# Four plain rows instead of six in a seven-product SwiGLU layer, with weight sums made by accumulating transfers

## The chip, the core and the metric

The kernel runs on one core of a Trainium2 chip. A core has five engines with queues of their own: TensorE (PE) multiplies, VectorE (DVE) and ScalarE (ACT) work on elements, GpSimd (POOL) here does little but issue transfers, and SyncE (SP) only issues transfers. The metric is device microseconds (us) from start to end; less is better. A measurement of this kernel can tell about 0.2% from no change, some 2.2 us.

## The reference, cut to what matters

One decoder layer is computed for 544 tokens (512 of a prompt, 32 of a decode step): a half-step SwiGLU feed-forward layer, a token mixer, and a second feed-forward layer of the same form with other weights. The change touches the two feed-forward layers only.

```python
def half_ffn(x, g_pre, g_post, w_gate, w_up, w_down):
    h = rmsnorm(x, g_pre)
    u = jax.nn.silu(h @ w_gate) * (h @ w_up)
    return x + 0.5 * rmsnorm(u @ w_down, g_post)
```

D_MODEL is 1024 (8 blocks of 128) and FFN_DIM is 2816 (22 blocks of 128), all in float32.

## The kernel before, in words

Everything lies transposed: features on the 128 partitions, the 544 tokens along the free dimension. A "row" is one block of 128 of the 2816 hidden features, so u has 22 rows. A float32 product is done in three passes of a reduced format: each operand is split into a high part (a cast on ACT) and a low part (a subtraction on DVE), and high x high, high x low and low x high are accumulated in PSUM.

Each feed-forward layer (`ffn`) makes its 22 rows in two ways.

*Plain rows* (PLAIN = 6 of them, rows 0 to 5): gate and up are two products over 8 blocks of the model dimension, for two token halves of 288 and 256 tokens. One such job (gate or up, one half) is 8 x 3 = 24 matmuls into a buffer `acc` of PSUM (three buffers), and a row has four jobs. `gate_out` multiplies the gate by the tokens' reciprocal norm `r` and applies silu; `upper_out` multiplies the up product by `r` and by the gate, and in the kernel before splits the result into the high and low parts that the down projection needs (lines 614 to 617), in SBUF.

*Pairs of rows* (`quadrants`, rows 6 to 21, so 8 pairs): gate and up of two rows together form a 2 x 2 block product (gate and up on one side against two halves of the model dimension, and two halves of 272 tokens on the other), done with seven products instead of eight (PRODUCTS, in the order 1, 5, 6, 2, 7, 3, 4). A product is 2 x 12 matmuls of 272 columns (two rows, 4 blocks, 3 passes), a pair 7 x 24 = 168. Four of the seven left factors are sums of the raw weights g0, g1 (the two halves of gate) and u0, u1 (of up): s3 = g0 + u0 for product 7, and u0 + u1, then + g0, then + g1 for products 5, 6 and 3. DVE makes all four, with `plus`. The right factors are seven combinations of the negated, normalised h, split into high and low parts (tiles `t` and `h`), made once for each layer by `right_parts` and `factors`. Before, ACT first scales X in place by the gain (line 422) and DVE by -r (line 429), and the parts come out of X.

The first pair must wait for its right factors. `ffn` therefore makes them in steps between the jobs of the plain rows (`steps`, `making`), and runs the last three jobs of the plain rows between the first products of the first pair (`beside`). So the plain rows are also the time in which DVE and ACT prepare the pairs. Weights are split one tile of 128 x 1024 at a time into a pool of three buffers; raw weights come by SP into a pool `raw` of two buffers, and the up weights of a pair into `rawx` or into the second half of X, in turn.

KEEP = 8 rows are multiplied with the down weights by seven products as well (`seven_down`), and the 14 others by three plain passes. Of the rows made by pairs, the first four pairs (rows 6 to 13) go out to DRAM (`u_keep`, by POOL) and come back later for `seven_down`.

The order on each engine is set when the program is built, by a list scheduler that goes by its own estimates of durations; each engine then runs its list strictly in order, so an instruction that waits holds up all behind it. A transfer's waits are held by the queue of the engine that issues it: POOL's list is in order too.

Of the kernel before, what the change touches and what calls it, by code (L numbers as in the profile page):

```python
# [39 lines left out]
WK = 4  # L40
# [3 lines left out]
PLAIN = 6  # L44
KEEP = 8

# [158 lines left out]
class _Builder:  # L205
# [202 lines left out]
    def u_tiles(self, li, ctx):  # L408

        t = ctx.enter_context(self.tc.tile_pool(name="u%d" % li, bufs=1)).tile([128, 2 * PLAIN, T], F32R, name="u%d" % li)  # L410
        return {m: (t[:, 2 * m, :], t[:, 2 * m + 1, :]) for m in range(PLAIN)}


    def right_parts(self, hs, gi, pool, behind):


        nc = self.nc
        X = self.X
        for k0 in range(0, KT, WK):
            with self.tc.issue_after(behind):  # L420
                for k in range(k0, k0 + WK):
                    nc.scalar.activation(out=X[:, k, :], in_=X[:, k, :], func=AF.Copy,
                                         scale=self.gain[:, gi * KT + k:gi * KT + k + 1])
            yield
        for half in range(2):
            r = self.rs(hs, half).unsqueeze(1).to_broadcast([128, WK, self.hw(half)])
            for k in range(0, KT, WK):
                x = X[:, k:k + WK, self.cols(half)]
                nc.vector.scalar_tensor_tensor(out=x, in0=x, scalar=-1.0, in1=r, op0=ALU.mult, op1=ALU.mult)
            yield  # L430
        h8 = self.h8, "h8"
        yield from self.factors({1: (pool, "t"), 5: (pool, "t"), 6: (pool, "t"), 2: h8, 7: h8, 3: h8, 4: h8})

    def factors(self, places):
# [3 lines left out]
        n11, n12, n21, n22 = (self.X[:, k:k + WK, c:c + HALF] for k in (0, WK) for c in (0, HALF))  # L438
# [81 lines left out]
    def quadrants(self, raws, small, put, beside, making):  # L520
# [4 lines left out]
        s3 = flat[:, 0:1024].rearrange("p (k m) -> p k m", k=WK)  # L525
# [6 lines left out]
        for u in range(PLAIN, KF, 2):  # L532
            (g0, g1), (u0, u1) = ((r[:, 0:WK], r[:, WK:KT]) for r in loaded)
            if PLAIN < u < KF - 2:
# [1426 lines left out]
```

## Time and profile before

| what | us |
|---|---|
| median of three runs | 1120.24 (1119.25 to 1120.26) |
| the profiled execution: its time | 1119.48 |
| the profiled execution: its span | 1117.7 |
| PE busy | 1100.3 (98%) |
| DVE busy | 845.0 (76%) |
| ACT busy | 632.8 (57%) |
| POOL busy | 124.7 (11%) |

In a timeline row the first number is the start in us from the beginning of the span, the second the length; then come engine, line of the program, operation, written tile <- read tiles, shape and count. Short instructions of one engine overlap at their ends, so the cost of one in a busy queue is the distance to the next start. A view of waits names who waited, for whom, the total, how often and the longest.

### The profile page before, as it was taken

To read this page: it belongs to the slowest core of one execution; us is meant where nothing else is said; L and a number is where in the kernel's file an instruction comes from. 1 tells how busy PE (TensorE), PEld (TensorE's weight loads), DVE (VectorE), ACT (ScalarE), POOL (GpSimd) and SP (SyncE) were. 2 spreads that over 40 slices of the span, in tenths; PEclk is the share of its full clock that TensorE was granted. 3 is DMA by queue.
4 is the path that set the end of the run, shared out by engine and by line. 5 is a ranking of instruction groups with operands and counts; after the bars stand their busy time and mean duration, and the time that the engine had idled before them with its cause. 6 is when DMAs were issued, how large, how long until landed. Compare 5 with 4: busy or idle time off the path is not lost.

```text
span 1117.7 us, 21930 instructions
## 1 busy us (share of the span) xinstructions
PE 1100.3 (98%) x8722; PEld 1063.1 (95%) x8722; DVE 845.0 (76%) x1716; ACT 632.8 (57%) x1368; POOL 124.7 (11%) x176
## 2 busy tenths in 40 slices
PE   9999999999999999999999899999999999999997
PEld 8999999999999999899889789999999999999997
DVE  5996787877875799658676478899787788787544
ACT  5844455555554656667564366776454455555444
POOL 0000000000000143521234432000000000000000
PEclk9999999999999999999999999999999999999999
DMA  9442344224245555643355546653333332243272
GB/s 269 143 133 94 116 134 130 80 66 153 71 150 172 153 146 143 189 132 91 92 158 172 170 126 203 203 177 110 114 127 118 132 101 91 89 133 95 82 212 80
DMA packets 150149, 149.47 MB, mean 134 GB/s; under 512 B 5965, under 2 KB 139189, under 8 KB 148512
## 3 DMA queue, kind: packets, MB, share of 16 engines
q1 hardware_dynamic: 135600, 100.55, 30.4%
q0 software_dynamic: 11504, 44.82, 11.9%
q10 hardware_dynamic: 2944, 2.71, 0.9%
q8 instruction: 68, 1.11, 0.4%
q14 instruction: 33, 0.27, 0.1%
HBM read 130.08 MB, written 18.51 MB: 133 GB/s over the span
## 4 chain that ended last, share of the span: by engine, by line
PE 81%; DVE 7%; issue 5%; ACT 3%; DMA 2%; POOL 1%; DVEq 0%; POOLq 0%; ACTq 0%; SPq 0%
PE acc L252 11%; PE acc L253 11%; PE acc L254 11%; PE acc L479 6%; PE acc L477 6%; PE acc L478 6%; PE aux L477 5%; PE aux L479 5%; PE aux L478 5%; PE smp L477 2%; PE smp L479 2%; PE smp L478 2%; DVE wl L241 2%; ACT wh L240 1%; PE smp L1357 1%
## 5 line engine op out<-in xcount | busy, mean ns | idle before, releaser
L240 ACT CAST wh<-raw 128x512 fp32r<-128x512 f32 (+2 forms) x281 | 183.3, 683 | 147.0 <-PE acc L253 62.8
L241 DVE TENSOR_TENSOR wl<-raw,wh 128x512 fp32r<-128x512 f32 (+2 forms) x281 | 209.2, 769 | 48.0 <-ACT wh L240 44.6
L252 PE MATMUL acc<-ha,wh 128*128 128x256 f32 (+1 forms) x576 | 166.3, 289 | 1.2 <-DVE rpost L614 1.2
L253 PE MATMUL acc<-ha,wh 128*128 128x256 f32 (+1 forms) x576 | 165.9, 288 | 0.0
L254 PE MATMUL acc<-ha,wl 128*128 128x256 f32 (+1 forms) x576 | 165.6, 287 | 0.0
L252 PE MATMUL acc<-h,wh 128*128 128x256 f32 (+1 forms) x552 | 164.2, 298 | 0.0
L253 PE MATMUL acc<-h,wh 128*128 128x256 f32 (+1 forms) x552 | 160.8, 292 | 0.0
L254 PE MATMUL acc<-h,wl 128*128 128x256 f32 (+1 forms) x552 | 160.0, 290 | 0.0
L252 PEld LDWEIGHTS acc<-h,wh 128*128 128x128 f32 x552 | 104.6, 190 | 7.7 <-issue 7.1
L252 PEld LDWEIGHTS acc<-ha,wh 128*128 128x128 f32 x576 | 108.8, 189 | 2.3 <-DVE rpost L614 1.4
L254 PEld LDWEIGHTS acc<-ha,wl 128*128 128x128 f32 x576 | 108.9, 189 | 0.0
L253 PEld LDWEIGHTS acc<-ha,wh 128*128 128x128 f32 x576 | 108.8, 189 | 0.1
L253 PEld LDWEIGHTS acc<-h,wh 128*128 128x128 f32 x552 | 104.7, 190 | 0.7 <-issue 0.4
L254 PEld LDWEIGHTS acc<-h,wl 128*128 128x128 f32 x552 | 104.4, 189 | 0.6 <-issue 0.4
L241 DVE TENSOR_TENSOR wl<-X,wh 128x1024 fp32r<-128x1024 f32 x48 | 58.8, 1224 | 26.5 <-ACT wh L240 26.5
L477 PE MATMUL acc<-h,wh 128*128 128x272 f32 x256 | 74.2, 290 | 0.0
L479 PE MATMUL acc<-t,wl 128*128 128x272 f32 x256 | 74.2, 290 | 0.0
L479 PE MATMUL acc<-h,wl 128*128 128x272 f32 x256 | 74.1, 289 | 0.0
L477 PE MATMUL acc<-t,wh 128*128 128x272 f32 x256 | 74.0, 289 | 0.0
L478 PE MATMUL acc<-t,wh 128*128 128x272 f32 x256 | 73.8, 288 | 0.0
L478 PE MATMUL acc<-h,wh 128*128 128x272 f32 x256 | 73.7, 288 | 0.0
L240 ACT CAST wh<-X 128x1024 fp32r<-128x1024 f32 x48 | 50.4, 1049 | 25.8 <-PE aux L478 14.8
(511 smaller groups left out, 3100.3 us busy)
## 6 DMA issues: line engine op xcount, KB each, us to landing
raw<-in_ffn_w_gate_dram SPq DMA_DIRECT2D x20, 1024.0 KB, 5.4
raw<-in_w_in_dram SPq DMA_DIRECT2D x28, 512.0 KB, 4.2
raw<-in_ffn_w_down_dram SPq DMA_DIRECT2D x21, 512.0 KB, 5.3
rawx<-in_ffn_w_up_dram SPq DMA_DIRECT2D x8, 1024.0 KB, 5.4
X<-in_ffn_w_up_dram SPq DMA_DIRECT2D x8, 1024.0 KB, 5.2
raw<-in_ffn_w_down_dram SPq DMA_DIRECT2D x8, 1024.0 KB, 5.7
raw<-in_ffn_w_down_dram SPq DMA_DIRECT2D x21, 384.0 KB, 3.8
raw<-in_w_out_dram SPq DMA_DIRECT2D x7, 1024.0 KB, 5.2
```

The costliest lines, as they stand in the source:

```text
L240: self.nc.scalar.copy(out=high, in_=src)
L241: self.nc.vector.tensor_tensor(out=low, in0=src, in1=high.bitcast(F32), op=ALU.subtract)
L252: nc.tensor.matmul(ps, lhsT=wh, rhs=xh(k0 + k), start=st, stop=False)
L253: nc.tensor.matmul(ps, lhsT=wh, rhs=xl(k0 + k), start=False, stop=False)
L254: self.last_mm = nc.tensor.matmul(ps, lhsT=wl, rhs=xh(k0 + k), start=False, stop=sp).ins
L477: nc.tensor.matmul(ps, lhsT=wh[:, k0 + k, cs], rhs=high[:, k, :], start=st, stop=False, skip_group_check=True)
L478: nc.tensor.matmul(ps, lhsT=wh[:, k0 + k, cs], rhs=low[:, k, :], start=False, stop=False, skip_group_check=True)
L479: self.last_mm = nc.tensor.matmul(ps, lhsT=wl[:, k0 + k, cs], rhs=high[:, k, :], start=False, stop=sp, skip_group_check=True).ins
L1357: nc.tensor.transpose(ps[:, h * 128:h * 128 + 128], kp[:, h * 128:h * 128 + 128], self.ident)
```

## The change

PLAIN goes from 6 to 4, so nine pairs take the place of eight. All four plain rows go out to DRAM as plain float32, half a row at a time: `upper_out` no longer splits its result but hands it to a transfer on POOL's queue (line 619), out of the small two-buffer pool tile `sqe` that the early gate also uses. Rows 0 to 7 (four plain rows and two pairs) now are the KEEP rows, and rows 8 to 13 take the place (`own`) that the plain rows had.

The normalised h gets a place of its own: DVE writes it from X with one operation per block of 128 features (line 423, X times `minus` times `r`), into the memory that later holds rows 8 to 13; ACT's scaling (line 422) is gone, and X keeps the raw input until it is used as a buffer. `r` is one tile for both halves. `minus` is the negated gain, made once on POOL.

Two of the four weight sums move to transfers. u0 + u1: after the load of the up weights, POOL issues a transfer that adds u1 from DRAM onto u0 in SBUF (line 706). s3 = g0 + u0: SP loads g0 into the place of s3 (line 713) and POOL adds u0 from DRAM onto it (line 714), one pair ahead. Both accumulating transfers bring 512 KB and wait on POOL for the load that they add to.

The making of the right factors is cut into three steps beside the plain rows (before, nine), and one step at each product of the first pair (before, all that was left at product 2).

The first place that moves is POOL's list in the first feed-forward layer. Before (x_ffn is the copy of X for the residual; bias_row and windows belong to the attention bias):

```order
L671 DMA x_ffn_586<-X_85 128x2176
L671 DMA x_ffn_586<-X_86 128x2176
L948 DMA bias_row<-xt 4x384
L951 DMA windows<-bias_row 512x1x256
L712 DMA u_keep_1042<-X_85 128x1088 x4
```

And now (u_keep<-sqe is half a plain row going out; the transfers from in_ffn_w_up_dram on this queue are the accumulating ones, X_85 being s3's place and X_86 the up weights of the second pair):

```order
L706 DMA rawx<-in_ffn_w_up_dram 128x4x256
L672 DMA x_ffn_583<-X_85 128x2176
L672 DMA x_ffn_583<-X_86 128x2176
L619 DMA u_keep_396<-sqe 128x288
L714 DMA X_85<-in_ffn_w_up_dram 128x4x256
L619 DMA u_keep_396<-sqe 128x256
L963 DMA bias_row<-xt 4x384
L966 DMA windows<-bias_row 512x1x256
L619 DMA u_keep_396<-sqe 128x288
L619 DMA u_keep_396<-sqe 128x256
L706 DMA X_86<-in_ffn_w_up_dram 128x4x256
```

The second half of row 0 (the 128x256 transfer behind the first one) now stands behind the accumulation onto s3, and both halves of row 1 behind windows.

The second place is DVE's list in the same layer, from row 1 on. Before:

```order
L241 TENSOR_TENSOR wl<-raw,wh 128x1024
L617 TENSOR_TENSOR u_99<-rpost,u_99 128x256
L598 TENSOR_TENSOR sq<-acc,r_460 128x288
L614 TENSOR_TENSOR rpost<-aux,r_460 128x288
L429 SCALAR_TENSOR_TENSOR X_86<-X_86,r_460 128x4x288
L615 TENSOR_TENSOR rpost<-rpost,sq 128x288
```

And now, with the semaphores that each waits for in brackets (DMASW is one of eight that POOL's transfers use in turn; here DMASW7 is the transfer of row 0's second half, DMASW2 that of row 1's first half; the number behind it is the same in all rows and says nothing):

```order
L242 TENSOR_TENSOR wl<-raw,wh 128x1024 [waits DMAHW4_49,Activation_49]
L609 TENSOR_TENSOR sq<-sq,sqe 128x288 [waits Activation_49]
L617 TENSOR_TENSOR sqe<-aux,r 128x288 [waits DMASW7_49,DVE_49]
L617 TENSOR_TENSOR sqe<-acc,r 128x256 [waits DVE_49]
L618 TENSOR_TENSOR sqe<-sqe,sq 128x288 [waits DVE_49]
L618 TENSOR_TENSOR sqe<-sqe,sq 128x256 [waits DVE_49]
L603 TENSOR_TENSOR sq<-acc,r 128x288 [waits PE_49]
L242 TENSOR_TENSOR t<-u,t 128x1088 [waits DMAHW5_49,DMASW1_49,DMAHW6_49,DMASW0_49,Activation_49]
L242 TENSOR_TENSOR wl<-raw,wh 128x1024
L617 TENSOR_TENSOR sqe<-acc,r 128x288 [waits DMASW2_49,DVE_49,PE_49]
```

The up product of row 1 (the two L617 next to each other) now has to wait until row 0's second half has left its buffer for DRAM, and that of row 2 (the last line) until row 1's first half has.

The third place is ACT's list in the first layer. Before, the gate's exponentials of rows 0 and 1 stand together and one table load follows (r_497 is the second half's norm):

```order
L601 ACTIVATE sqe<-sq 128x288
L603 ACTIVATE sqe<-sqe 128x288
L602 ACTIVATE sqe<-sqe 128x288
L279 ACTIVATE r_497<-r_497 128x256
L603 ACTIVATE sqe<-sqe 128x288
L240 CAST wh<-raw 128x1024
L616 CAST u_99<-rpost 128x288
L606 ACT_TABLE_LOAD
```

And now:

```order
L608 ACTIVATE sqe<-sqe 128x288
L611 ACT_TABLE_LOAD
L611 ACTIVATE sq<-sq 128x256
L606 ACT_TABLE_LOAD
L606 ACTIVATE sqe<-sq 128x288
L611 ACT_TABLE_LOAD
L611 ACTIVATE sq<-sq 128x256
L607 ACT_TABLE_LOAD
L607 ACTIVATE sqe<-sqe 128x288
L241 CAST wh<-raw 128x1024
L608 ACT_TABLE_LOAD
L608 ACTIVATE sqe<-sqe 128x288
```

Silu (L611) of the second half and the exponentials of row 1 (L606 to L608) alternate, each with a table load of its own; another load before the next silu makes six where there was one. The second layer has one in both.

The diff, cut to its core:

```diff
-PLAIN = 6
+PLAIN = 4
 KEEP = 8
+OWN = 6
...
-            r = self.rp.tile([128, HA], F32, name="r%d" % half)[:, 0:self.hw(half)]
+            if hs[1 - half][3] is None:
+                self.r = self.rp.tile([128, T], F32, name="r")
+            r = self.r[:, self.cols(half)]
...
+    def right_parts(self, gi, place, pool):
+        nc = self.nc
+        n = place.tile([128, 2 * OWN, T], F32, name="u")[:, 0:KT]
+        def scaled(k0):
+            for k in range(k0, k0 + WK):
+                nc.vector.scalar_tensor_tensor(out=n[:, k, :], in0=self.X[:, k, :],
+                                               scalar=self.minus[:, gi * KT + k:gi * KT + k + 1], in1=self.r,
+                                               op0=ALU.mult, op1=ALU.mult)
+        scaled(0)
+        yield
+        h8 = self.h8, "h8"
+        making = self.factors({1: (pool, "t"), 5: (pool, "t"), 6: (pool, "t"), 2: h8, 7: h8, 3: h8, 4: h8}, n)
+        for _ in range(2):
+            next(making)
+        yield
+        scaled(WK)
+        yield from making
...
             for p in PRODUCTS:
-                if u == PLAIN and p == 2:
-                    _run(making)
-                    loaded = raws(u + 2)
-                if p == 5:
-                    plus(s3, g0, u0)
-                    plus(u0, u0, u1)
-                elif p == 6:
+                if u == PLAIN:
+                    next(making, None)
+                    if p == 5:
+                        loaded = raws(u + 2)
+                if p == 6:
                     plus(u0, u0, g0)
...
                 self.parts(src, *w)
+                if p == 7 and u < KF - 2:
+                    s3 = both(u + 2)
...
-                uu = self.tmp.tile([128, HA], F32, name="rpost", bufs=1)[:, 0:self.hw(half)]
+                uu = self.tmp.tile([128, HA], F32, name="sqe")[:, 0:self.hw(half)]
                 nc.vector.tensor_tensor(out=uu, in0=pu, in1=self.rs(hs, half), op=ALU.mult)
                 nc.vector.tensor_tensor(out=uu, in0=uu, in1=sg, op=ALU.mult)
-                nc.scalar.copy(out=uh[:, sl], in_=uu)
-                nc.vector.tensor_tensor(out=ul[:, sl], in0=uu, in1=uh[:, sl].bitcast(F32), op=ALU.subtract)
+                nc.gpsimd.dma_start(out=spill[:, m, self.cols(half)], in_=uu)
...
-            steps = 4 + 5
+            steps = 3
...
-                for r, w in zip((g, u), views):
-                    nc.sync.dma_start(out=r, in_=w[:, :, m * 128:m * 128 + 256])
+                vg, vu = (w[:, :, m * 128:m * 128 + 256] for w in views[:2])
+                nc.sync.dma_start(out=g, in_=vg)
+                nc.sync.dma_start(out=u, in_=vu)
+                nc.gpsimd.dma_start(out=u[:, 0:WK], in_=vu[:, WK:KT], accum_op=ALU.add)
                 return g, u
...
+            def both(m):
+                s3 = self.X.tiles[0].rearrange("p k t -> p (k t)")[:, 0:1024].rearrange("p (k m) -> p k m", k=WK)
+                vg, vu = (w[:, 0:WK, m * 128:m * 128 + 256] for w in views[:2])
+                nc.sync.dma_start(out=s3, in_=vg)
+                nc.gpsimd.dma_start(out=s3, in_=vu, accum_op=ALU.add)
+                return s3
...
-            groups = [(0, PLAIN), (PLAIN + KEEP, KF - PLAIN - KEEP)]
+            groups = [(KEEP, OWN), (KEEP + OWN, KF - KEEP - OWN)]
...
+        nc.gpsimd.tensor_scalar_mul(self.minus, self.gain, -1.0)
```

More of the change, by code (lines that the diff above doesn't have):

```diff
@@ L408, in u_tiles, with factors @@
     def u_tiles(self, li, ctx):
-        t = ctx.enter_context(self.tc.tile_pool(name="u%d" % li, bufs=1)).tile([128, 2 * PLAIN, T], F32R, name="u%d" % li)
-        return {m: (t[:, 2 * m, :], t[:, 2 * m + 1, :]) for m in range(PLAIN)}
-    def right_parts(self, hs, gi, pool, behind):
+        return ctx.enter_context(self.tc.tile_pool(name="u%d" % li, bufs=1))
+    def right_parts(self, gi, place, pool):
         nc = self.nc
[L418 to L423, printed above, removed]
-            yield
[L425 to L434, printed above, removed]
+        n = place.tile([128, 2 * OWN, T], F32, name="u")[:, 0:KT]
[10 more added lines that the diff above has]
+            next(making)
+            yield
+        scaled(WK)
+        yield from making
+    def factors(self, places, n):
         nc = self.nc
         self.t = t = {}
-        n11, n12, n21, n22 = (self.X[:, k:k + WK, c:c + HALF] for k in (0, WK) for c in (0, HALF))
+        n11, n12, n21, n22 = (n[:, k:k + WK, c:c + HALF] for k in (0, WK) for c in (0, HALF))
         def parts(p, src):
@@ L518, in seven_down, with quadrants @@
                 nc.scalar.copy(out=x1[:, C0], in_=ps)
-    def quadrants(self, raws, small, put, beside, making):
+    def quadrants(self, raws, both, small, put, beside, making):
         nc = self.nc
         flat = self.X.tiles[0].rearrange("p k t -> p (k t)")
-        s3 = flat[:, 0:1024].rearrange("p (k m) -> p k m", k=WK)
         uu = flat[:, 1024:1024 + 2 * T].rearrange("p (a t) -> p a t", a=2)
@@ L591, in ffn @@
         with ExitStack() as ctx:
-            rows = u or self.u_tiles(li, ctx)
+            own = u if u is not None else self.u_tiles(li, ctx)
+            rows = {}
             sgs = {}
+            spill = tc.dram_tile([128, KEEP, T], F32, name="u_keep%d" % li)
             def gate_out(pg, m, half, early=False):
@@ L700, in raws @@
                     u = small.tile([128, 8, 256], F32, name="rawx")
[L701 to L702 removed]
+                vg, vu = (w[:, :, m * 128:m * 128 + 256] for w in views[:2])
+                nc.sync.dma_start(out=g, in_=vg)
+                nc.sync.dma_start(out=u, in_=vu)
+                nc.gpsimd.dma_start(out=u[:, 0:WK], in_=vu[:, WK:KT], accum_op=ALU.add)
                 return g, u
[L704 to L707 removed]
+            def both(m):
[4 more added lines that the diff above has]
+                return s3
             def put(m, uu):
[L710 to L714 removed]
+                if m < KEEP:
+                    nc.gpsimd.dma_start(out=spill[:, m:m + 2, :], in_=uu)
+                else:
+                    i = 2 * (m - KEEP)
+                    if i == 0:
+                        self.own = own.tile([128, 2 * OWN, T], F32R, name="u")
+                    if i < 2 * OWN:
+                        s = self.own[:, i:i + 4].rearrange("p (a b) t -> p a b t", a=2)
+                    else:
+                        s = self.ha.tile([128, 2, 2, T], F32R, name="ha")
                     self.parts(uu, s[:, 0], s[:, 1])
                     rows.update({m + a: (s[:, 0, a, :], s[:, 1, a, :]) for a in range(2)})
[L717 removed]
+            self.quadrants(raws, both, small, put, beside(), making)
             more.__exit__(None, None, None)
@@ L725, in ffn @@
             places = {p: (late, "late%d_%d" % (li, p)) for p in (1, 5, 6, 2)}
-            own = [self.h8.tile([128, 2, WK, HALF], F32R, name="h8") for _ in range(2)]
-            places[7], places[3] = lambda: own[0], lambda: own[1]
+            free = [self.h8.tile([128, 2, WK, HALF], F32R, name="h8") for _ in range(2)]
+            places[7], places[3] = lambda: free[0], lambda: free[1]
             places[4] = lambda: self.x_tile(0, (128, 2, WK, HALF), F32R)
-            making = self.factors(places)
+            making = self.factors(places, self.X)
             last_x = late.tile([128, tail - 2, T], F32, name="x%d" % li)
```

20 lines of the change are left out of this document (6 added, 14 removed).

## The prediction

> **What bounds the kernel now.** I read the page first, its busy times and the chain that ended last.
>
> ```profile
> PE 1100.3 (98%) x8722; PEld 1063.1 (95%) x8722; DVE 845.0 (76%) x1716; ACT 632.8 (57%) x1368; POOL 124.7 (11%) x176
> ...
> PE 81%; DVE 7%; issue 5%; ACT 3%; DMA 2%; POOL 1%; DVEq 0%; POOLq 0%; ACTq 0%; SPq 0%
> ```
>
> PE is busy for 98% of the span and carries the chain. So only two things count: fewer columns for PE, and new times in which PE waits. DVE at 76% looks free, but that is a mean over stages. I therefore took a table of stretches next: twice two stretches of plain rows, one of each layer, and between them a pair in the steady loop. The columns are stretch, length, PE, PEld, DVE, ACT, POOL busy, granted clock, DMA share and GB/s.
>
> ```profile
> 48.00:60.00 12.00, 10.83 (x88) 10.63 (x87) 12.00 (x18) 7.07 (x11) 0.00 (x0) 1.00 0.62 207
> 60.00:72.00 12.00, 12.00 (x98) 12.00 (x97) 12.00 (x19) 6.75 (x10) 0.00 (x0) 1.00 0.01 4
> 113.10:134.30 21.20, 21.20 (x170) 21.20 (x169) 16.78 (x22) 10.68 (x17) 0.55 (x1) 1.00 0.38 127
> ...
> 761.00:773.00 12.00, 12.00 (x96) 11.84 (x96) 12.00 (x19) 7.68 (x11) 0.00 (x0) 1.00 0.30 93
> 773.00:785.00 12.00, 12.00 (x99) 12.00 (x98) 12.00 (x18) 5.65 (x8) 0.00 (x0) 1.00 0.24 84
> ```
>
> In the steady pair DVE has 4.4 of 21.2 us to spare. While plain rows run it has nothing: 12.00 of 12.00 in both layers, because it also makes the right factors then. In the first layer PE even stood still once, as the view of waits shows (total, how often, longest):
>
> ```profile
> PE acc L252 <- DVE rpost L614: 1.2, 1, 1.2
> ```
>
> The change takes plain rows away, so it shortens just this stretch.
>
> **What PE gains.** In PE's timeline, first matmuls of jobs of the plain rows, then the first product of the first pair in either layer; and POOL's sends of finished pairs:
>
> ```profile
> 68.04 0.29 PE L252 MATMUL acc<-ha,wh 128*128 128x288 f32 x1
> ...
> 74.39 0.28 PE L252 MATMUL acc<-ha,wh 128*128 128x256 f32 x1
> ...
> 79.99 0.29 PE L252 MATMUL acc<-ha,wh 128*128 128x288 f32 x1
> ...
> 83.17 0.29 PE L477 MATMUL acc<-t,wh 128*128 128x272 f32 x1
> ...
> 797.58 0.29 PE L477 MATMUL acc<-t,wh 128*128 128x272 f32 x1
> ```
>
> ```profile
> 135.36 0.54 POOL L712 DMA_DIRECT2D u_keep<-X  x1 [20.36 <-DVE X L574]
> 156.55 0.53 POOL L712 DMA_DIRECT2D u_keep<-X  x1 [20.66 <-DVE X L574]
> ```
>
> A plain row is 79.99 - 68.04 = 11.95 us: two jobs of 288 columns take 6.35 (3.18 each), two of 256 take 5.60 (2.80 each). A pair is 156.55 - 135.36 = 21.19, a product a seventh of it, 3.03. Two plain rows out and a pair in give 21.19 - 23.90 = **-2.71 us in a layer, -5.42 in all**, if PE never waits. The down projection keeps 14 plain rows and 8 by seven products, so it is unchanged.
>
> **What DVE is left with.** Before the first pair stand 20 us more of cover than after, in jobs 13 before and 5 now (three more between products in both). The distance from one DVE start to the next in a full queue is the price of an operation:
>
> ```profile
> 36.27 0.46 DVE L598 TENSOR_TENSOR sq<-acc,r 128x288 f32<-128x288 f32 x1
> ...
> 42.09 0.45 DVE L617 TENSOR_TENSOR u<-rpost,u 128x288 fp32r<-128x288 f32 x1
> 42.46 1.22 DVE L429 SCALAR_TENSOR_TENSOR X<-X,r 128x1024 f32<-128x1024 f32 x1
> 43.60 0.42 DVE L614 TENSOR_TENSOR rpost<-acc,r 128x256 f32<-128x256 f32 x1
> 43.93 0.54 DVE L946 COPY xt<-aux 4x384 f32<-4x384 f32 x1
> 44.40 0.40 DVE L615 TENSOR_TENSOR rpost<-rpost,sq 128x256 f32<-128x256 f32 x1
> ...
> 49.92 1.29 DVE L241 TENSOR_TENSOR t<-X,t 128x1088 fp32r<-128x1088 f32 x1
> 51.12 0.45 DVE L617 TENSOR_TENSOR u<-rpost,u 128x288 fp32r<-128x288 f32 x1
> ```
>
> So 1088 elements cost 1.20, 1024 cost 1.14, 288 cost .37, 256 cost .33, the small copy .47; 544 lie between 288 and 1024, by a straight line .64. What goes from this stretch is two rows' weight splits (4 x 1.14), their four small operations per half (about 5.6), eight low parts of u (8 x .35 = 2.8) and two sums (2.3): about 15 us of DVE, against 23.9 us of PE. A stretch that was full becomes tighter by about 9.
>
> **First layer, the demand.** The second product of the first pair (number 5) needs its weights when PE gets there. Product 1 would start at 83.17 - 23.90 = 59.27; product 1 and two jobs beside follow: 59.27 + 3.03 + 3.18 + 2.80 = 68.28. I take this product because nearly all right factors stand ahead of its weights in DVE's list.
>
> **First layer, the supply.** DVE begins the rows at 36.27 as before. Seven small operations (2.53) and four of the new 544 ones (2.56) bring it to 41.36; four more of 544, two small ones and the copy (3.70) to row 1's weight split at 45.06. That split needs ACT's cast, which the new order of silu and exponentials holds up:
>
> ```profile
> 37.47 0.43 ACT L602 ACTIVATE sqe<-sqe 128x288 f32<-128x288 f32 x1
> 37.81 0.44 ACT L601 ACTIVATE sqe<-sq 128x288 f32<-128x288 f32 x1
> ...
> 41.27 1.28 ACT L606 ACT_TABLE_LOAD   x1
> ...
> 43.19 1.03 ACT L240 CAST wh<-raw 128x1024 fp32r<-128x1024 f32 x1
> 44.13 1.39 ACT L422 ACTIVATE X<-X,gain 128x544 f32<-128x544 f32 x2
> ```
>
> A small ACT operation costs .34, a table load 1.28, the cast .94. Four loads with four functions take 6.4 and stand ahead of the cast: ACT would come to it at 44.4 and end it at 45.35, so the split ends at 46.5, and another load and function let row 1's gate be done at 47.35. DVE then has 21.2 us of work up to the weights of product 5 (10 x 1.20, 4 x 1.14, 8 x .37, 5 x .335): 68.55 with no further wait, and PE, which starts on it .25 before (the high part comes first), wants it at 68.53. **The margin is nothing**, so each further wait of DVE reaches PE. ACT has half of that stretch free and is not counted again.
>
> **First layer, the new waits.** Row 1's up (the two L617) cannot start until row 0's second half has left its buffer. That transfer is on POOL's queue behind the accumulation onto s3. No row shows an accumulating transfer. The nearest rows are these (KB each, median us from issue to landing):
>
> ```profile
> raw<-in_w_in_dram SPq DMA_DIRECT2D x28, 512.0 KB, 4.2
> ```
>
> ```profile
> X<-u_keep POOLq DMA_DIRECT2D x4, 1088.0 KB, 5.3
> windows<-bias_row POOLq DMA_DIRECT2D x1, 512.0 KB, 5.9
> out_dram<-vas_tok POOLq DMA_DIRECT2D x1, 64.0 KB, 2.4
> rawx<-in_ffn_w_up_dram SPq DMA_DIRECT2D x1, 1024.0 KB, 8.7
> ```
>
> s3's load can issue at 41.35, when X's first half is free, and lands 4.2 later, 45.55. The accumulation cannot land sooner than 4.2 after that, as a plain load of its 512 KB; above, it reads 512 KB from DRAM and 512 in SBUF, for which 5.3 (1088 KB on this queue) is nearest, and twice a plain load is 8.4. I take 5.3: it lands at 50.85. Row 0's half issues at 46.1. Below, it overtakes and lands 2.4 later at 48.5; above, it comes in order, .5 behind the accumulation, at 51.35. Against DVE's 47.35 that is a wait of 1.15 to 4.0; I take 4.0, since both go through the same queue and this is a queue of one list. Row 2's up waits in turn for row 1's first half, which is queued behind windows (5.9): DVE would come there at 55.5, the transfer lands at 54.6 to 57.9, a wait of 0 to 2.4; I take 2.4. Behind the waiting L617 stands everything DVE does for the factors, and PE waits for that. Sum of lateness 6.4: the layer gives -2.71 + 6.4 = **+3.7** (with the lower ends -1.6; with 8.4 for the accumulation 6.8).
>
> The Trainium skill, "DMA: Bandwidth & Descriptors", section "Anatomy of one DMA — SWDGE (gpsimd) path", puts a transfer at 2.0 us plus its bytes over 436 GB/s: 3.2 us for 512 KB, and none for an accumulation; for the 1088 KB it gives 4.6 where the trace shows 5.3. By it row 0's half would be there about 49.2, the wait 1.9 instead of 4.0 and, as an estimate, the kernel at about 1119.8.
>
> **Second layer.** There is no bias transfer there, ACT has one table load as before, and DVE comes to row 1's up at about 757.6, with the first layer's operations from here:
>
> ```profile
> 755.46 0.42 DVE L598 TENSOR_TENSOR sq<-acc,r 128x256 f32<-128x256 f32 x1
> ...
> 744.17 0.37 SPq L702 DMA_DIRECT2D rawx<-in_ffn_w_up_dram  x1
> ```
>
> The spill it waits for is behind the accumulation onto the first pair's up weights: their load issues at 744.17, lands 8.7 later (752.9), plus 5.3 and .5 makes 758.7, a wait of 1.1. From there DVE has 25.0 us (9 x 1.20, 5 x 1.14, 6 x .64, 8 x .37, 5 x .335), ending at 783.7; PE wants it at 797.58 - 23.90 + 9.01 + .25 = 782.95. Late by .7: **-2.0** (from -2.7 without a wait to +2.5 with 8.4).
>
> **What costs nothing, and its cover.** In the steady pairs both sums leave DVE. For s3, product 7's parts of the pair before must be made first; needed is it one pair later at the cast:
>
> ```profile
> 119.33 1.05 ACT L240 CAST wh<-X 128x1024 fp32r<-128x1024 f32 x1 [1.05 <-PE aux L478]
> ```
>
> ```profile
> 120.41 1.23 DVE L241 TENSOR_TENSOR wl<-X,wh 128x1024 fp32r<-128x1024 f32 x1 [0.66 <-ACT wh L240]
> ```
>
> Load 121.64 + 4.2 = 125.9, cast 119.33 + 21.19 = 140.5: 14.6 us for a transfer that I price at 5.3, at most 8.4. Without that cover each of 16 pairs waits for what is over. ACT's scaling by the gain (eight of about .7 a layer) was off the chain and goes; the additional pair's casts and splits lie under its own 21.2 us of PE, DVE being at 16.78 there and now 2.3 lower.
>
> **Sum.** +3.7 - 2.0 = +1.7 on the profiled execution's 1119.48 us (span 1117.7, 1.8 around it): 1121.2. That execution lies .76 below the median of the runs, so on the median's scale **1121.9**.
>
> **Rivals.** *The small transfers overtake.* If a half row leaves within 2.4 us whatever stands ahead of it, DVE waits 1.15 only: -1.6 - 2.7 = -4.3, **1116**. For it: the half row's 147 KB need none of the accumulation's data, and 16 DMA engines serve the queue. Against: the queue is one list in order. No row shows two overlapping transfers on POOL's queue with the landings of each. The same page of the Trainium skill, section "Queues, rings and completion order", has a ring's descriptors consumed in order while completions can come out of order: it excludes neither.
>
> *The accumulation is slow.* At 8.4 us, twice a plain load, the lateness grows to +6.8 and +2.5: +9.3, **1129.5**. It decides from about 6.5 us for 512 KB. For it: 1 KB pieces read twice and written once, and a load of 1024 KB that took 8.7 in the stretch it meets. Against: 5.2 to 5.4 for the loads of that size elsewhere, while the DMA share is .01 to .62 here.
>
> *The waits are absorbed.* DVE waits as I say, but `acc` has three buffers and the products of the first pair take turns with jobs beside, so 2 to 3 us of 7.1 don't reach PE: about 1119. Against: the stretch has no idle DVE time in which to catch up.
>
> *The accumulation takes more than 14.6 us.* Then every pair waits for s3 on ACT, and PE behind it: above 1140. Nothing in the rows points so far.
>
> **How the numbers follow.** My forecast .38; overtaking .30; slow .15; absorbed .13; far slower .04. The least that this measurement can tell is about .2%, 2.2 us: same is 1118.0 to 1122.5. The forecast's own spread is some 3 us to either side, so I split it: .06 faster, .17 same, .15 slower. Overtaking gives .28 faster and .02 same; absorbed .03 and .10; the two slow ones .19 slower. Faster .37, same .29, slower .34. The range 1115.5 to 1129 leaves out the far slow case, half of the slow one, and little of the rest.
>
> **What will show it.** In the profile after: DVE's L617 waiting for u_keep<-sqe between 47 and 58, about 4.0 and 2.4 us, and once about 758, 1.1; PE's waits for DVE's wl or t between 62 and 72 and near 782, 6.4 and .7 in sum; sends of pairs still 21.19 apart; the accumulating transfers about 5.3 to landing; six table loads early on ACT. If DVE's L617 don't wait, the queue does not hold the spills, and the first rival is right; if accumulations need over 6.5, the second. The forecast is wrong altogether if PE's idle time in these two stretches is below 3 or above 12 us.

## The result, and the profile after

The changed kernel takes 1128.2 us (median of 4, 1126.39 to 1131.14) against 1120.25 for the kernel before: a ratio of 1.0070, 95% interval 1.0054 to 1.0086. It is slower by 8 us. The forecast was 1121.9 with a range of 1115.5 to 1129, so the time lies in the range, near its upper end; nearest to it of the rivals' numbers is that of the slow accumulation, 1129.5. Being slower by more than 2.2 us had .34 of the chances, and faster .37.

The page of the changed kernel, busy times and the chain that ended last:

```profile
PE 1094.0 (97%) x8674; PEld 1056.5 (94%) x8674; DVE 817.8 (73%) x1678; ACT 637.2 (57%) x1357; POOL 176.9 (16%) x225
...
PE 81%; DVE 8%; DMA 6%; issue 2%; ACT 2%; POOL 1%; DVEq 0%; ACTq 0%; SPq 0%; POOLq 0%
```

PE has 6.3 us less to do (1100.3 before), DVE 27 us less, and still the span is 6.9 us longer. In the chain DMA has gone from 2% to 6%: PE now waits for something that a transfer holds up. Two sends on POOL's queue mark the stages: the first x_keep is the end of the first feed-forward layer, the first x_ffn behind it the start of the second. Before:

```profile
377.80 0.78 POOL L1654 DMA_DIRECT2D x_keep<-X  x1 [30.46 <-DVE X L360]
...
739.95 0.56 POOL L671 DMA_DIRECT2D x_ffn<-X  x1 [30.31 <-DVE X L360]
```

And after:

```profile
381.78 0.77 POOL L1669 DMA_DIRECT2D x_keep<-X  x1 [30.35 <-DVE X L363]
...
746.88 0.56 POOL L672 DMA_DIRECT2D x_ffn<-X  x1 [30.31 <-DVE X L363]
```

So the first layer is 4.0 us longer, the mixer between them (which the change doesn't touch) 2.9, and the second layer the same (1124.6 - 746.88 = 377.7 against 377.75). The view of PE's waits of the changed kernel, for the whole span:

```profile
PE acc L479 <- ACT wh L241: 5.4, 1, 5.4
PE smp L1372 <- DMA pgin<-in_cache_k_dram,idx: 2.6, 1, 2.6
PE acc L255 <- DVE wl L242: 2.5, 2, 1.3
PE acc L481 <- DVE wl L242: 2.3, 1, 2.3
...
PE acc L253 <- DVE sqe L617: 0.5, 1, 0.5
```

The second row belongs to the mixer (before it had one of 2.8). The others lie in the plain rows and at the first product: 5.4 (the first product), 1.2 and .5 (plain rows) in the first layer, 1.3 (a plain row's weights) and 2.3 (the first product, whose low part DVE makes late) in the second. Beside them the steady pairs are what they were; the stretch of 130 us in the first layer's loop before, and now:

```profile
100.00:230.00 130.00, 130.00 (x1033) 130.00 (x1032) 105.77 (x125) 67.53 (x107) 2.15 (x4) 1.00 0.38 121
```

```profile
100.00:230.00 130.00, 130.00 (x1034) 130.00 (x1033) 95.92 (x116) 70.26 (x111) 15.97 (x13) 1.00 0.75 181
```

PE does the same number of matmuls without a gap. DVE has 10 us less there. But the DMA engines' share has doubled, .38 to .75.

The longest wait is followed back through four timelines of the changed kernel. DVE, the up products that wait for the transfers of the small tile (in brackets the idle time and what ended it):

```profile
42.57 0.42 DVE L617 TENSOR_TENSOR sqe<-acc,r 128x256 f32<-128x256 f32 x1 [0.99 <-DMA u_keep<-sqe]
...
46.39 0.46 DVE L609 TENSOR_TENSOR sq<-sq,sqe 128x288 f32<-128x288 f32 x1
49.20 0.46 DVE L617 TENSOR_TENSOR sqe<-aux,r 128x288 f32<-128x288 f32 x1 [2.35 <-DMA u_keep<-sqe]
...
54.89 0.46 DVE L617 TENSOR_TENSOR sqe<-acc,r 128x288 f32<-128x288 f32 x1 [1.50 <-DMA u_keep<-sqe]
...
766.86 0.46 DVE L617 TENSOR_TENSOR sqe<-aux,r 128x288 f32<-128x288 f32 x1 [3.22 <-DMA u_keep<-sqe]
```

POOL, the accumulation onto s3 and the spill behind it; in the second layer the accumulation onto the up weights and its spill:

```profile
42.73 1.33 POOL L714 DMA_DIRECT2D X<-in_ffn_w_up_dram  x1 [3.42 <-DMA X<-in_ffn_w_gate_dram]
44.08 0.56 POOL L619 DMA_DIRECT2D u_keep<-sqe  x1
...
760.22 1.34 POOL L706 DMA_DIRECT2D rawx<-in_ffn_w_up_dram  x1 [8.40 <-ACT r L279]
761.02 1.13 POOL L619 DMA_DIRECT2D u_keep<-sqe  x1
```

The 128 KB spill of 44.08 lets DVE go on at 49.20: 5.1 us, behind an accumulation that began 6.5 us before that. In the second layer the two stand 6.6 apart. Then the second pair's accumulation on POOL's queue, SP's queue (one row for three issues, the first at 53.46), where the first pair's gate load has to wait for a weight buffer that DVE frees, ACT's cast of it, and PE's first product:

```profile
52.55 1.34 POOL L706 DMA_DIRECT2D X<-in_ffn_w_up_dram  x1 [0.81 <-ACT sq L611]
```

```profile
53.46 29.80 SPq L703 DMA_DIRECT2D raw<-in_ffn_w_gate_dram  x3
```

```profile
63.41 1.04 ACT L241 CAST wh<-raw 128x1024 fp32r<-128x1024 f32 x1 [5.40 <-DMA raw<-in_ffn_w_gate_dram]
```

```profile
64.50 0.60 PE L479 MATMUL acc<-t,wh 128*128 128x272 f32 x1 [5.41 <-ACT wh L241]
```

The load of 1024 KB, 5.4 us in the median before, takes 9.95 here (53.46 to 63.41), and PE stands for it. What stands then is the clock; a table of stretches around it, with the granted clock as the third number from the end:

```profile
63.00:66.00 3.00, 1.50 (x6) 1.44 (x7) 1.52 (x3) 2.04 (x2) 0.00 (x0) 0.50 0.75 251
66.00:70.00 4.00, 4.00 (x23) 4.00 (x23) 4.00 (x5) 1.12 (x3) 0.00 (x0) 0.64 0.00 0
```

From 64.5 on PE works at .50; the .64 is a mean over 66 to 70, for the matmuls' distance falls back to that of full speed at 68.9. That is 1.5 x .50 + 4 x .36 = 2.2 us lost on top of the wait. The Trainium skill, "TensorE: Matmul & The Clock Gate", section "What's actually happening", has the clock at half after an idle window of about 3.4 us until a busy one has passed; this trace agrees in kind: in slices of 1 us the clock falls at about 62.0, 2.9 us after PE's last matmul, and is back at 68.9, 4.4 us after product 1 began. The wait of 2.3 us in the second layer has no such price: the clock stays at 1.00 behind it.

What an accumulation does to the DMA engines is seen in slices of .25 us from 42 to 52 us (busy tenths of the engines, and GB/s); the accumulation moves from about 45 to 47.7, plain transfers behind it:

```profile
DMA  0000000000096899999999999999999999999989
GB/s 0 0 0 0 0 0 0 0 0 0 0 66 66 98 160 147 160 197 197 197 197 197 197 270 340 345 361 389 393 381 381 385 365 360 348 344 287 344 311 393
```

All 16 engines are busy in both, but the accumulation moves 197 GB/s and the plain transfers up to 393. The Trainium skill, "Collectives: The Full Stack", section "The bandwidth ceiling: the fold count and why AG ≠ RS ≠ AR", says of a collective's ReduceScatter that it isn't slow by the adding but because the add reads two sources through the same ring, which halves the rate. The trace agrees in the rate, 197 against 393; no run here shows the reads.

### The profile page after: what moved, and what is told of

Its sections match the earlier page's. It is cut to its first block, busy times and chain, and to the rows that moved or that the text cites. A ratio compares the mean times of both kernels' runs of the same rounds, so it can differ in the third digit from the quotient of the medians.

```text
span 1124.6 us, 21965 instructions
## 1 busy us (share of the span) xinstructions
PE 1094.0 (97%) x8674; PEld 1056.5 (94%) x8674; DVE 817.8 (73%) x1678; ACT 637.2 (57%) x1357; POOL 176.9 (16%) x225
## 3 DMA queue, kind: packets, MB, share of 16 engines
q10 hardware_dynamic: 2944, 2.71, 0.8%
## 4 chain that ended last, share of the span: by engine, by line
PE 81%; DVE 8%; DMA 6%; issue 2%; ACT 2%; POOL 1%; DVEq 0%; ACTq 0%; SPq 0%; POOLq 0%
PE acc L253 10%; PE acc L254 10%; PE acc L255 10%; PE acc L479 7%; PE acc L481 6%; PE acc L480 6%; PE aux L479 5%; PE aux L480 5%; PE aux L481 5%; PE smp L480 2%; PE smp L479 2%; PE smp L481 2%; DVE wl L242 1%; DMA raw<-in_ffn_w_gate_dram 1%; DMA u_keep<-sqe 1%
## 5 line engine op out<-in xcount | busy, mean ns | idle before, releaser
L242 DVE TENSOR_TENSOR wl<-raw,wh 128x512 fp32r<-128x512 f32 (+2 forms) x277 | 204.1, 762 | 51.2 <-ACT wh L241 47.9
L255 PE MATMUL acc<-ha,wl 128*128 128x256 f32 (+1 forms) x448 | 129.3, 289 | 2.5 <-DVE wl L242 2.5
L253 PE MATMUL acc<-ha,wh 128*128 128x256 f32 (+1 forms) x448 | 129.7, 289 | 0.5 <-DVE sqe L617 0.5
L254 PE MATMUL acc<-ha,wh 128*128 128x256 f32 (+1 forms) x448 | 129.4, 289 | 0.0
L479 PE MATMUL acc<-t,wh 128*128 128x272 f32 x288 | 84.0, 292 | 5.4 <-ACT wh L241 5.4
L255 PEld LDWEIGHTS acc<-ha,wl 128*128 128x128 f32 x448 | 85.0, 190 | 2.9 <-DVE wl L242 2.9
L253 PEld LDWEIGHTS acc<-ha,wh 128*128 128x128 f32 x448 | 85.1, 190 | 1.5 <-DVE sqe L617 0.7
L481 PE MATMUL acc<-t,wl 128*128 128x272 f32 x288 | 84.0, 292 | 2.3 <-DVE wl L242 2.3
L254 PEld LDWEIGHTS acc<-ha,wh 128*128 128x128 f32 x448 | 85.0, 190 | 0.1
L480 PE MATMUL acc<-h,wh 128*128 128x272 f32 x288 | 83.6, 290 | 0.0
L480 PE MATMUL acc<-t,wh 128*128 128x272 f32 x288 | 83.4, 290 | 0.0
L481 PE MATMUL acc<-h,wl 128*128 128x272 f32 x288 | 83.0, 288 | 0.0
L479 PE MATMUL acc<-h,wh 128*128 128x272 f32 x288 | 82.9, 288 | 0.0
L242 DVE TENSOR_TENSOR wl<-rawx,wh 128x1024 fp32r<-128x1024 f32 x40 | 49.0, 1226 | 30.4 <-ACT wh L241 30.4
```

Source lines behind the costliest of these rows:

```text
L242: self.nc.vector.tensor_tensor(out=low, in0=src, in1=high.bitcast(F32), op=ALU.subtract)
L253: nc.tensor.matmul(ps, lhsT=wh, rhs=xh(k0 + k), start=st, stop=False)
L254: nc.tensor.matmul(ps, lhsT=wh, rhs=xl(k0 + k), start=False, stop=False)
L255: self.last_mm = nc.tensor.matmul(ps, lhsT=wl, rhs=xh(k0 + k), start=False, stop=sp).ins
L479: nc.tensor.matmul(ps, lhsT=wh[:, k0 + k, cs], rhs=high[:, k, :], start=st, stop=False, skip_group_check=True)
L480: nc.tensor.matmul(ps, lhsT=wh[:, k0 + k, cs], rhs=low[:, k, :], start=False, stop=False, skip_group_check=True)
```

## The experiments

Two causes stood side by side after the traces. **Q**: the spills stand in POOL's queue behind accumulations, and DVE, with nothing to spare, is late by what they wait. **L**: the accumulations take the DMA engines at half rate, and the first pair's gate load lands late. Rivals were **C**, that four plain rows are too little cover for DVE in any case, and **S**, that accumulations cost something beside the steady pairs too. Each kernel was timed beside the kernel before on the same chip; since chips differ by some us (the one of the version with SP's spills ran the kernel before in 1116.8), ratios to it are compared. 1% is 11.2 us. The change itself is at 1.0070 and, in a second measurement, 1.0064.

**Both sums back on DVE, for all pairs.**

```diff
-                if p == 6:
+                if p == 5:
+                    plus(s3, g0, u0)
+                    plus(u0, u0, u1)
+                elif p == 6:
...
-                nc.gpsimd.dma_start(out=u[:, 0:WK], in_=vu[:, WK:KT], accum_op=ALU.add)
...
-                nc.sync.dma_start(out=s3, in_=vg)
-                nc.gpsimd.dma_start(out=s3, in_=vu, accum_op=ALU.add)
```

> The changed kernel with both weight sums back on DVE for all pairs (s3 and u0 + u1 made at product 5), four plain rows, their spills as in the change. Nothing is left out of the computation. Theory Q and L (spills wait in POOL's queue behind accumulations, and the accumulations slow the first pair's gate load, 9.85 us instead of 5.4): DVE's waits for u_keep<-sqe fall from 4.8 and 3.2 us to under 1.5 in each layer, the gate load lands in about 5.5 us, PE waits under 3 us in each first pair, and the time is 1115 to 1119. Rival C (four plain rows are too little cover for DVE, whatever the queues do): DVE has 2.3 us more to do before product 5, PE still waits 5 us or more in each layer, and the time is 1125 to 1130.

1115.8 us, ratio .9955 (.9940 to .9970): 12 us below the change and 5 below the kernel before. DVE's waits for spills are .3 and .6 us, the gate load issued at 51.39 is cast at 57.69 (6.3 us), and PE waits 1.9 us in the first layer up to and in its first pair, and 1.2 in the second's. Rival C falls: with four plain rows and 2.3 us more of DVE work, DVE is in time. What it does not say is which of Q and L paid.

**Free slots instead of the small tile** (no wait for a spill; accumulations stay).

```diff
-                uu = self.tmp.tile([128, HA], F32, name="sqe")[:, 0:self.hw(half)]
+                uu = wide[:, KT + m, self.cols(half)]
...
+            wide = own.tile([128, 2 * OWN, T], F32, name="u")
```

> The changed kernel, with the plain rows' up product written into the four free slots of the place that later holds rows 8 to 13 instead of the two-buffer tile, so that no operation waits for a spill; the accumulating transfers stay. Nothing is left out. Theory Q: DVE's waits for spills (4.8 and 3.2 us) are gone, and the first pair's gate load can issue some 3.3 us earlier; the time falls by 5 to 9 us to 1119 to 1123. Theory L: the load still takes about 10 us beside the accumulations and PE still waits 2 to 5 us before the first product; if only the load counts, the time stays at 1126 to 1129. Rival C: PE waits as long as before for DVE's weights, 1126 to 1129 as well, but DVE shows no idle time.

1120.1 us, .9995 (.9986 to 1.0004): 8 us below the change. DVE no longer waits for spills, the gate load issues 3.55 us earlier (49.91), and PE waits 1.2 and 1.5 us at the first pair. The trace is of the slowest of its eleven executions, in which PE waits 3 us for the input at the start, so 3.55 is too little rather than too much. Theory Q's numbers came.

**The spills issued by SP instead of POOL** (small tile and accumulations stay).

```diff
-                nc.gpsimd.dma_start(out=spill[:, m, self.cols(half)], in_=uu)
+                nc.sync.dma_start(out=spill[:, m, self.cols(half)], in_=uu)
```

> The changed kernel with the plain rows' spills issued by SP instead of POOL; the two-buffer tile and all accumulating transfers stay. Nothing is left out. Theory Q in the form that the order in POOL's queue holds the spills: DVE's waits for u_keep<-sqe (4.8 to 5.4 us in the first layer, 3.2 to 3.4 in the second) fall below 1.5 us in each layer, the gate load still lands late, and the time is near that with the free slots, 1119 to 1122. The other form, that spills are late because the accumulations occupy the DMA engines whatever the queue: the waits stay at 3 us or more in each layer and the time at 1126 to 1129.

1.0036 (1.0024 to 1.0049), 3 to 4 us below the change by the ratio (the times themselves are of the chip with 1116.8). DVE's waits in the first layer, of this kernel and of the change:

```profile
DVE sqe L617 <- DMA u_keep<-sqe: 2.4, 2, 1.8
```

```profile
DVE sqe L617 <- DMA u_keep<-sqe: 4.8, 3, 2.3
```

Half is left (and 1.3 of 3.2 in the second layer). Neither form of the expectation holds alone: about half of the spills' delay goes with the order of POOL's queue, the rest stays on another queue. That it stays because the accumulation occupies the engines is likely, but not shown apart from SP's own loads. The gate load is no longer slow: 6.9 us from its issue at 53.32 to its cast at 60.21. An accumulation was issued .46 us before it here too, but that one landed only after 10.4 us. So an accumulation issued near a load does not by itself make the load late, and the gain of this version is not Q's alone.

**The same transfers without the addition** (so the sums are not made).

```diff
-                nc.gpsimd.dma_start(out=u[:, 0:WK], in_=vu[:, WK:KT], accum_op=ALU.add)
+                nc.gpsimd.dma_start(out=u[:, 0:WK], in_=vu[:, WK:KT])
...
-                nc.gpsimd.dma_start(out=s3, in_=vu, accum_op=ALU.add)
+                nc.gpsimd.dma_start(out=s3, in_=vu)
```

> The changed kernel with the addition left out of the accumulating transfers: the same transfers overwrite instead of adding, so the sums are not made and the values of the pairs are not the layer's. Theory L in the form that the addition halves the rate of a transfer: 512 KB go at nearly 400 GB/s instead of some 195, the spill behind lands 1.5 us sooner, the gate load lands in 6 to 8 us, and the time is 1122 to 1126. If the order in the queue and the number of bytes are all that counts, it stays at 1127 to 1129.

1123.3 us, 1.0023 (1.0012 to 1.0034): 5 us below the change, for the same bytes from DRAM. The first product starts at 61.61 instead of 64.50, and PE's wait there is 1.5 instead of 5.4. DVE's waits for spills are 5.9 and 3.9 us in the two layers, no less in sum, but in the first layer they moved: the one right behind the transfer onto s3 shrank from 2.35 to .83 us, and the next one, for a spill behind windows, grew from 1.50 to 4.23:

```profile
47.66 0.46 DVE L617 TENSOR_TENSOR sqe<-aux,r 128x288 f32<-128x288 f32 x1 [0.83 <-DMA u_keep<-sqe]
...
56.08 0.46 DVE L617 TENSOR_TENSOR sqe<-acc,r 128x288 f32<-128x288 f32 x1 [4.23 <-DMA u_keep<-sqe]
```

So the addition feeds both causes. The gate load issues 1.55 us earlier (51.91), which is Q's part, and its cast comes 8.6 us after that instead of 9.95, which is L's; the 6 to 8 us expected were not reached. In this kernel the DMA engines move 393 GB/s between 45.5 and 46.0 us, while only POOL's queue moves data: the 197 of the change go with the addition, not with the bytes or the queue. How the 5 us divide between the two causes, this run does not say: the profiled execution is the slowest of its twelve (1126.76).

**Only the first pair's sums on DVE**, later pairs by transfers.

```diff
-                nc.gpsimd.dma_start(out=u[:, 0:WK], in_=vu[:, WK:KT], accum_op=ALU.add)
+                if m > PLAIN:
+                    nc.gpsimd.dma_start(out=u[:, 0:WK], in_=vu[:, WK:KT], accum_op=ALU.add)
```

(and s3 in the same way)

> The changed kernel with DVE making both sums of the first pair alone; the eight later pairs of each layer keep their accumulating transfers (the second pair's first one still falls beside the plain rows). Nothing is left out. Theory F (what the accumulations cost is paid at the first pair alone): as with all sums on DVE, which took 1115.8, within 2 us: 1115 to 1118. Rival S (accumulations beside the steady pairs cost too, as the 1124.5 with six plain rows would suggest): half or more of the 12 us between this and the change stays, 1121 to 1126.

1121.7 us, 1.0008 (.9993 to 1.0023), 6 us above the version with all sums on DVE. That looked like S. The trace puts it elsewhere: the second pair's accumulation issues at 50.06, still beside the plain rows, and the first pair's gate load, issued at 51.11, is cast only at 60.49:

```profile
ACT wh L241 <- DMA raw<-in_ffn_w_gate_dram: 6.2, 1, 6.2
...
PE acc L479 <- ACT wh L241: 3.6, 1, 3.6
```

9.4 us for the load as in the change, without any wait for a spill: this is L by itself.

**Free slots, and the first pair's sums on DVE**: the diff of the free slots and the one just above together.

> The up products of the plain rows in the free slots (no wait for a spill) and the first pair's sums on DVE; later pairs by accumulating transfers. Nothing is left out. The version with the slots and all accumulations took 1120.1. Theory L (the first pair's accumulations slow its gate load and hold the queue): 1114 to 1117. Rival S: 1118 to 1121.

1115.5 us, .9957 (.9937 to .9977), single runs from 1109.6 to 1122.4. The trace shows one more place of Q: the first pair's send behind the next accumulations. POOL's timeline, and DVE, which needs the place that is sent:

```profile
91.76 1.31 POOL L711 DMA_DIRECT2D rawx<-in_ffn_w_up_dram  x1 [9.98 <-DVE wl L242]
92.54 1.11 POOL L724 DMA_DIRECT2D u_keep<-X  x1
```

```profile
102.41 0.79 DVE L531 TENSOR_TENSOR X<-smp,p 128x272 f32<-128x272 f32 x2 [4.72 <-DMA u_keep<-X]
```

Almost 10 us for a send whose median was 3.0 before.

**Free slots, sums on DVE for three pairs, accumulations for the six later ones.** As the kernel just above, with another condition.

```diff
-                if m > PLAIN:
+                if m > PLAIN + 4:
```

> The up products of the plain rows in the free slots, DVE making both sums of the first three pairs, and accumulating transfers for the six later pairs of each layer, so that none of them is near the plain rows or ahead of the sends of the first two pairs. Nothing is left out. Theory F (accumulations cost only where something waits: the first pair's loads, spills and sends): the version with all sums on DVE, 1112.5, within 1 us. Rival S (accumulations beside steady pairs cost as such): 1114.5 or more, and single runs spread by 5 us or more.

1114.0 us, .9929 (.9912 to .9946), and the version with no accumulation at all, below, is at .9930. Theory F holds and S falls: 24 of the 36 transfers are still there, and cost nothing once no load, spill or send that something waits for is near them. They bring nothing either.

**Free slots, and all sums on DVE**: the first and the second diff together.

> The up products of the plain rows in the free slots and all sums on DVE: four plain rows without a wait for spills and without accumulations. Nothing is left out. If the two causes are all that kept the gain away: PE loses less than 2 us in each first pair; the kernel before less 5.4 us, 1113 to 1116. If cover is short after all (rival C), DVE still is late by some 3 us in each layer and the time is 1117 to 1120.

1112.45 us (1112.14 to 1114.02), .9930 (.9915 to .9945): it beats both kernels, 8 us below the kernel before. PE does not wait at all at the first layer's first pair, and .8 us at the second's. DVE is full in the first layer, 12.00 and 11.70 of 12 us, and still in time:

```profile
48.00:60.00 12.00, 12.00 (x99) 12.00 (x98) 12.00 (x17) 5.99 (x8) 1.10 (x2) 1.00 0.82 254
60.00:72.00 12.00, 12.00 (x100) 12.00 (x99) 11.70 (x13) 5.95 (x9) 0.54 (x1) 1.00 0.26 90
```

**The same with the first two rows' gates by exponentials**, so that one table load stands early on ACT where three did.

```diff
-            gate_out(ps[0], 0, 1)
+            gate_out(ps[0], 0, 1, True)
...
-            gate_out(ps[2], 1, 1)
+            gate_out(ps[2], 1, 1, True)
```

> The version before this one, with the first two rows' gates all made by exponentials in the first and the second layer, so that one table load stands early on ACT where that version has three. Nothing is left out. If ACT's table loads hold up row 1 and with it DVE and PE: 1 to 2 us less than the version before this one. If row 1's weights wait for something else, no change (within 0.8 us); two more multiplications on DVE cost .7 us a layer at worst.

1113.4 us, .9933 (.9916 to .9949): no change. In the version without waits the table loads are not what row 1 waits for.

**Six plain rows in the change.**

```diff
-PLAIN = 4
+PLAIN = 6
```

> The changed kernel with six plain rows and eight pairs again, all the rest as in the change (rows 0 to 7 are the rows kept in DRAM, six of them plain). Nothing is left out. All three theories of the first pair (queue, load, cover): with 20 us more of plain rows before the first product PE waits under 2 us there, and the time is that of the kernel before, 1118 to 1122. Rival S (the accumulating transfers also cost something beside the steady pairs, or elsewhere): it stays above 1124.

1124.5 us, 1.0035 (1.0021 to 1.0049). In the first layer DVE still waits 5.2 us for spills; PE waits 1.9 and 2.5 us in the two layers, 4.4 in all, and all of it in the plain rows (46.65, 50.40 and 764.85); at the first product it does not wait. So 20 us more of cover do spare the first pair, as expected, but not the rows themselves from the queue. The time is the one that the expectation gave to S; the run with accumulations for the six later pairs alone speaks against S.

**Six plain rows with both sums on DVE.**

> The change with both sums on DVE and six plain rows instead of four, so that it stands to the run with all sums on DVE (1115.8) only by the two rows and the pair. Nothing is left out. If the two rows are worth what the prediction gave, 5.4 us less what PE waits at the first pair: 1118 to 1121. If six plain rows with accumulations took 1124.5 because of the accumulations, this one is 3 to 6 us below that; if because of the spills or the new place, it stays at 1123 to 1125.

1121.7 us, 1.0005 (.9993 to 1.0017), just above the expected 1118 to 1121. Against the run with four plain rows and all sums on DVE (.9955) it gives the worth of the two rows and the pair by itself: .50%, 5.6 us, by the two intervals good to some 2 us. Against the six plain rows with accumulations (1.0035) it gives 3.4 us for the accumulations with much cover.

**The change once more.**

> The changed kernel itself, unaltered, on the same chip as the two others, with a second trace. The first two rows' waits for spills (4.8 and 3.2 us), the load of the first pair's gate (9.85 us) and PE's wait before product 1 (5.4 us) should come back within 1 us each, if the order of the queues sets them; the mixer, 3 us longer in the first trace than in the kernel before, should come back within 1 us of the kernel before if that was chance. Time 1127 to 1130.

1128.7 us, 1.0064 (1.0049 to 1.0079). DVE waits 5.4 and 3.4 us for spills, the load takes 9.4 us, PE waits 4.7 us before the first product. The mixer is 364.85 us long (747.12 - 382.27), 2.7 above the kernel before: the expectation that this was chance fell.

## Why the prediction was right, and where its steps failed

The time lies in the range, but the forecast was +1.7 us for the profiled execution and +6.9 was measured. Of the 5.2 between, the mixer has 2.9, the second layer 2.0 and the first layer .3; the first layer came that near by luck, as shown below.

**The gain of PE's work, -2.71 a layer: right.** 5.6 us, good to some 2, between the two runs with all sums on DVE that differ only by it (estimate 5.42), and the steady pairs are unchanged.

**DVE's margin of nothing: right.** With free slots and no accumulations DVE fills the stretch and PE waits for .8 us in all; with the waits, PE waits too.

**The spills behind the accumulation: right in kind, and the first rival wrong.** They do not overtake. The waits were priced at 6.4 us in the first layer and measured at 4.8 and 5.4: row 1's was 2.35 where 4.0 was priced, row 2's 1.50 where 2.4 was, and .99 at row 0 had no term. The load of s3's place issued at 38.13 instead of 41.35, so the accumulation began at 42.73, 2.8 us before the 45.55 of the forecast; that hid that it is slower than priced. In the second layer 1.1 was priced and 3.2 measured: the accumulation and the spill behind it took 6.6 us where I had 5.8, and DVE came 0.9 earlier than I had (756.7 on the time of the trace before, where the forecast has 757.6). The nearest row, 5.3 for a plain transfer of 1088 KB, was too low by a good 1 us: an accumulation moves at half rate. The slow accumulation was to decide from about 6.5 us; it is about there. Its number has a slip: with 8.4 for 5.3 the second layer's wait grows by 3.1 to 4.2, its lateness to 3.8, and the layer to +1.1, not +2.5, so that this rival would have stood at 1128.1.

**The step that failed is the demand.** I took product 5's weights as the first thing that PE would miss, "because nearly all right factors stand ahead of its weights in DVE's list". What it missed was product 1's: their gate load waits for a weight buffer that the late DVE frees (3.3 us late by then), and lands in 9.95 us instead of 5.4, beside a second accumulation that was issued at 52.55. From 57 to 60 us, while both are under way, the DMA engines move 226 to 239 GB/s in all. The prediction has no term for loads that accumulations slow. It cost PE 5.4 us and then 2.2 of clock, and the sum of the first layer came near (+3.7 forecast, +4.0 and +4.5 measured) only because two things went the other way: PE is through the work ahead of the plain rows earlier (the job that begins at 42.58 before begins at 41.39, 1.2 us earlier), and the 1.2 us that PE waited for rpost before are gone. With the measured terms the layer is -2.7 - 1.2 - 1.2 + 7.1 (PE's waits) + 2.2 (clock) = +4.2, against +4.0 in that trace. The forecast had only the first term and 6.4 for the waits, so that it came near is luck. The second layer's -2.0 became 0 and .1 by the spill's 3.2: PE waits 3.6 us there, where .7 was forecast, and there too at product 1 and before it (2.3 us at 784.03 for product 1's low part, 1.3 at 769.57 for a plain row's), not at product 5.

**ACT's six table loads: a wrong worry.** They were in the supply's chain for .85 us; with one load for three, in the version without waits, nothing changed. For the change itself no run tests them.

**The steady pairs: right.** The sums lie under 14.6 us of cover, and six pairs of accumulations cost nothing. The rival of over 14.6 us falls with it. That the waits would be absorbed falls too.

**The mixer: not forecast, and open.** Its 2.9 and 2.7 us are over a third of the result. Its instructions stand in the same order as before. It was 362.2 us in the kernel before, 362.0 to 363.9 in most variants, and near 365 in the change, in its repeat, in the version with free slots and in that without the addition; the kernel with SP's spills, on another chip, has 360.4 with all the accumulations. Two pieces can be read in the traces. In all four near 365 the granted clock falls once in the mixer, which loses 1.7 us (.83 over 440 to 450 us in the change, .83 over 640 to 650 in free slots and without the addition, .84 and .99 over 640 to 660 in the repeat). It does so in the version with the first pair's sums on DVE as well (363.7), and in the kernel before (.94 and .89 over 630 to 650), and in none of the others. And PE waits 1.0 to 1.6 us for DVE's X in every version but that with SP's spills, and not in the kernel before. What sets either is not shown, and no run was made that would.

## What to carry to other kernels

A transfer that adds takes work off an engine that has time, and puts it on queues: look first which loads, spills and sends stand behind it or beside it, and price it at half the rate of a plain one. Where an engine is full in a stretch (12.00 of 12.00), any new wait in its list can reach the bottleneck, as the spills' did here, and a buffer that is free anyway is worth more than the operations saved: the four free slots gave 8 us (under 3 where no accumulation stands in the queue, .9955 against .9930), the sums taken off DVE in the steady pairs none. In a forecast, follow each load that the late engine releases, up to its first user, and not only that engine's own list.

## What the runs showed of the hardware that I had not expected

An accumulation of 512 KB keeps all 16 DMA engines busy at 197 GB/s, where plain transfers move up to 393, and the transfer behind it on the same queue is done 6.5 to 6.6 us after the accumulation is issued. A load of 1024 KB takes 9.4 to 9.95 us instead of 5.4 when an accumulation was issued just before it (the change, its repeat, the first pair's sums on DVE); with the spills on SP's queue it took 6.9, and the accumulation 10.4. With no accumulation in the kernel it took 6.3 in the same stretch. After a stall of 5.4 us the granted clock is .50 from about 62.0 to 68.9. After one of 2.6 us (in the version with SP's spills, first product at 61.31) it was .50 from 63.5 to 66.9 too, though that wait is shorter than the idle window of about 3.4 us that the Trainium skill, "TensorE: Matmul & The Clock Gate", section "What's actually happening", names. After 2.3 us in the change's second layer (784.03) it stayed at 1.00: at such lengths the wait alone does not tell whether the clock falls.
